# Spreading 48 row sums evenly over a hybrid encoder block, and splitting one job's first weights earlier

## The chip, the cores and the metric

The kernel runs on one core of one Trainium2 chip. A core has five engines that run side by side and wait for one another through semaphores: TensorE (PE: matmuls, with PEld its weight loads), VectorE (DVE), ScalarE (ACT), GpSimd (POOL) and SyncE (SP, which here only issues DMAs). The metric is the device time of one execution in microseconds, the median of several runs; lower is better.

## The reference

The reference is one layer of a bidirectional hybrid encoder block on 256 tokens of width 2048, all in fp32. A conditioning vector c gives six rows of modulation, and these are what the change is about:

```python
mod = silu(c) @ ada_w + ada_b                    # ada_w: 2048 x 12288
shift_m, scale_m, gate_m, shift_f, scale_f, gate_f = split(mod, 6)
h = rms_norm(x, norm_mix_w) * (1 + scale_m) + shift_m
proj = h @ w_in                                  # 2048 x 18512, split into the branches
y_a = (sigmoid(a_o) * rms_norm(mlstm(...))) @ w_branch_a   # 4 heads, both directions
y_b = (rms_norm(gated_delta(...)) * silu(b_z)) @ w_branch_b # 16 heads, both directions
x = x + gate_m * ((g_a * y_a + g_b * y_b) @ w_out)
hf = rms_norm(x, norm_ffn_w) * (1 + scale_f) + shift_f
x = x + gate_f * ((silu(hf @ w_gate) * (hf @ w_up)) @ w_down)
return rms_norm(x, norm_final_w)
```

Shift and scale of the mixer (parts 0 and 1 of mod) are needed at once; gate_m (part 2) after both branches, shift_f and scale_f (parts 3 and 4) before the FFN, gate_f (part 5) at the end.

## The kernel before

All weights are streamed from HBM once, in chunks of 1 MB. A chunk lands in one of three raw buffers. Half of it at a time is split into a rounded high part wh (a copy on ScalarE) and the rest wl (a subtraction on VectorE), three buffers each; TensorE then does three products per block, wh with the high activations, wh with the low ones, wl with the high ones. A job is a Python generator that does one such half per step: fjob (L173) for 128 output columns, two steps; tjob (L199) for 512 output columns, eight steps. A list called fills holds the jobs that aren't urgent, and fill(n) runs n of their steps; the latency chains of the two branches put such steps between their own.

The parts 2 to 5 of mod aren't computed on TensorE. For each of 16 blocks of a part a transposed block of ada_w, 128 rows of 2048 numbers (1 MB), is loaded (ask, L111) and multiplied with the row silu(c) and summed along the row in one VectorE instruction (add, L120). ask puts its load in SyncE's queue, the one that also loads the weight chunks. I call such an instruction a sum. Parts 2, 3 and 4 are 48 sums and are queued at L1016; part 5 is 16 sums during the FFN.

When a sum is traced is decided in pump (L157), which every step of every job calls. It has two ways. With the one buffer of the pool rows_p, a step asks for a load if none is out; a later step adds it if a sum is owed, more than two steps have gone by since the load, and the sums aren't held. With the variable every at 1 a sum is owed at each step, so this comes to one sum every four steps. The other way is taken while room (L108) names a pool of three buffers: then every fourth step traces one sum, and the loads run up to three ahead.

The stages in order, with what the sums do in them:

- start: norm, the first projections, and the gates; no sums of this kind.
- groups g = 0 to 3 of four gated-delta heads. For each, gdn_invert inverts small triangular blocks on VectorE (no sums), then come gdn_blocks and two pairs of heads, gdn_phase2 (L749), a chain of nine steps each, with the q, k, v jobs of the next group (b_job) and fills between the steps (L1040 on). every is 1 in these pairs, and the sums are held in steps 1 to 3 of a pair. A pair's last step transposes its output on TensorE (px), evicts it on ScalarE (obt) and stores it. After group g the job z of group g + 1 is put ahead of the fills (L1060), and the next inversion runs.
- in group 3 mLSTM heads 0 and 1 are begun; then every is set to 0 (L1121), and these heads end amid the y_b jobs. every is 1 again (L1147) for mLSTM heads 2 and 3, still amid y_b.
- y_a, four jobs, with room naming three buffers of a new pool sr and every at 4. That pool also holds gm and the products of row_diag (L1159), from which gate_m is spread over all partitions. merged (L1103) transposes the merged branches.
- the output jobs o, four, with sums called by hand at two steps of each and the rest of them at one step of the last (L1312). Then the FFN.

What order the engines run in is not the order of the program. The framework's planner simulates the program and gives each engine a fixed order: of the instructions that it believes ready, the one that was traced first. An instruction in order(...) is pinned behind the one traced before it on its engine. Functions in the list behind (settle, L139) are traced at the next half of a job; among them are the copies of a head's diagonal corners (corners, L676).

Of the kernel before, what the change touches and what calls it, by code (L numbers as in the profile page):

```python
# [15 lines left out]
P = 128  # L16
# [36 lines left out]
def hybrid_block(ctx: ExitStack, tc: tile.TileContext, xr, nfr, crow, pk_d, cst_d, ada2, ada4, win0, winb, wint, wba, wbb, wo, wgu, wd, out, dbg=None):  # L53
# [54 lines left out]
    room = [(rows_p, "ada", 1, 1)]  # L108
    asked, unasked, age = [], [], [0]

    def ask():  # L111

        pl, tag, bufs, _ = room[0]
        part, b = unasked.pop(0)
        raw = pl.tile([P, D], F32, tag=tag, bufs=bufs, name=f"ada{part}_{b}")
        order(nc.sync.dma_start(raw, ada4[part - 2, b]))
        asked.append((part, b, raw))
        age[0] = 0
# [80 lines left out]
    def tjob(name, chunks, xh, xl, done, early=0, by_token=None, steps=1, parts=((0, slice(0, 512)), (1, slice(0, 512)))):  # L199
# [7 lines left out]
        def halves(u, k0):  # L207
# [5 lines left out]
            order(S.activation(wh, raws[u][:, k0 : k0 + 2], AF.Copy), early)  # L213
            settle()
            order(V.tensor_tensor(wl, raws[u][:, k0 : k0 + 2], wh.bitcast(F32), ALU.subtract), early)  # L215
# [150 lines left out]
    def z_job(g, early=0):  # L366
# [4 lines left out]
        return tjob(f"z{g}", [wint[g, u] for u in range(4)], hh, hl, done, early)  # L371
# [654 lines left out]
    for g in range(4):  # L1026
# [94 lines left out]
    every[0] = owed[0] = 0  # L1121
# [25 lines left out]
    every[0] = 1  # L1147
# [32 lines left out]
    every[0] = 4  # L1180
    for g in range(4):
        for i, _ in enumerate(y_a(g)):
            if g and i == 3:
                merged(g - 1, mgh, mgl)
            if i in (1, 5) and g < 2:
                row_diag(2, 2 * g + i // 4, room[0][0])
            if i in (3, 7) and g < 2:
                row_spread(2, 2 * g + i // 4, gm)
    every[0] = 0
# [128 lines left out]
    room[0] = (rows_p, "ada", 1, 1)  # L1318
# [244 lines left out]
```

## Time and profile before

| | us |
|---|---|
| median of three runs | 1973.17 |
| lowest and highest | 1971.56, 1974.83 |
| the profiled execution | 1974.3 |
| its span, first to last instruction | 1972.4 |

The profile is of one execution. Its page gives busy times and their shares of the span; a chain of work, followed back from the last instruction to what released it; and groups of equal instructions with their count, mean duration in ns, and the idle time of the engine ahead of them. Other views answer from the same trace: who waited for whom, the instructions of one engine in order of time (start, length, engine, line, operation, with the idle time before it and its releaser in brackets), and windows with the busy time of each engine. SPq and ACTq rows are DMA issues of those queues, and their length reaches from the first to the last of the count. The end of a matmul is modelled, so matmuls overlap in these rows, and their rate is read from the starts.

### The profile page before, as it was taken

The numbers are of one execution on the slowest core, as the hardware profiler recorded it, in microseconds if no ns is written. First come the engines' busy times: TensorE is split into PE (matmuls) and PEld (weight loads), VectorE is DVE, ScalarE is ACT, GpSimd is POOL, SyncE is SP. The second block draws the span as 40 slices with busy tenths as digits, with TensorE's granted clock in tenths as the row PEclk, the third lists the DMA queues.
The fourth block names the chain that finished last, engine by engine and source line by source line (L and its number), as shares of the span: only waits on it lengthen the run. The fifth ranks groups of instructions, "written<-read, shape, count | busy, mean of one in ns | idle before, by whom it ended". The sixth has DMA issues, their size and how long they took to land.

```text
span 1972.4 us, 27079 instructions
## 1 busy us (share of the span) xinstructions
PE 1929.4 (98%) x10418; PEld 1703.5 (86%) x10418; DVE 1405.5 (71%) x2067; ACT 1030.0 (52%) x1555; POOL 116.5 (6%) x211
## 2 busy tenths in 40 slices
PE   8999999999999999999999999999999999999998
PEld 6878889998998899889787888888888888888886
DVE  6779887887888798866577878866665665555554
ACT  3137656764766577565544444644444444444444
POOL 0001210111001010110100000200000000000000
PEclk9999999999999999999999999999999999999999
DMA  9987676766566666586777888566676665565663
GB/s 399 420 349 226 184 249 240 252 214 208 203 217 213 237 218 229 192 296 246 277 282 266 323 317 330 191 252 238 238 265 241 237 238 205 197 213 197 208 199 142
DMA packets 78962, 485.64 MB, mean 246 GB/s; under 512 B 10585, under 2 KB 15969, under 8 KB 24433
## 3 DMA queue, kind: packets, MB, share of 16 engines
q1 hardware_dynamic: 63216, 450.69, 62.9%
q0 software_dynamic: 8160, 17.88, 4.5%
q10 hardware_dynamic: 7458, 15.36, 2.1%
q8 instruction: 81, 1.33, 0.3%
q14 instruction: 47, 0.39, 0.1%
HBM read 467.07 MB, written 16.82 MB: 245 GB/s over the span
## 4 chain that ended last, share of the span: by engine, by line
PE 81%; DVE 8%; DMA 6%; ACT 2%; issue 1%; POOL 0%; ACTq 0%; SPq 0%; DVEq 0%; POOLq 0%
PE acc_gt L234 4%; PE acc_gt L235 4%; PE acc_gt L236 4%; PE acc_up L236 4%; PE acc_up L235 4%; PE acc_up L234 4%; PE acc_d L236 4%; PE acc_d L235 4%; PE acc_d L234 4%; DMA ra<-ada 3%; PE acc_b L187 2%; PE acc_b L188 2%; PE acc_b L189 2%; PE acc_o L236 2%; PE acc_o L234 2%; PE acc_o L235 2%
## 5 line engine op out<-in xcount | busy, mean ns | idle before, releaser
L215 DVE TENSOR_TENSOR wl_d<-raw_d,wh_d 128x1024 fp32r<-128x1024 f32 x88 | 107.7, 1224 | 105.9 <-ACT wh_d L213 105.9
L215 DVE TENSOR_TENSOR wl_up<-raw_up,wh_up 128x1024 fp32r<-128x1024 f32 x88 | 107.7, 1224 | 100.2 <-ACT wh_up L213 100.1
L215 DVE TENSOR_TENSOR wl_gt<-raw_gt,wh_gt 128x1024 fp32r<-128x1024 f32 x88 | 108.1, 1229 | 80.2 <-ACT wh_gt L213 80.2
L187 PE MATMUL acc_b<-hh,wh_b 128*128 128x256 f32 x576 | 163.0, 283 | 0.6 <-ACT wh_b L182 0.6
L189 PE MATMUL acc_b<-hh,wl_b 128*128 128x256 f32 x576 | 159.6, 277 | 0.8 <-DVE wl_b L184 0.8
L188 PE MATMUL acc_b<-hl,wh_b 128*128 128x256 f32 x576 | 159.2, 276 | 0.0
L213 ACT ACTIVATE wh_d<-raw_d 128x1024 fp32r<-128x1024 f32 x88 | 92.9, 1056 | 126.5 <-PE acc_d L235 117.7
L213 ACT ACTIVATE wh_gt<-raw_gt 128x1024 fp32r<-128x1024 f32 x88 | 92.9, 1056 | 118.6 <-PE acc_gt L235 71.1
L213 ACT ACTIVATE wh_up<-raw_up 128x1024 fp32r<-128x1024 f32 x88 | 92.8, 1055 | 108.1 <-PE acc_up L235 77.1
L124 DVE SCALAR_TENSOR_TENSOR ada<-ada,crow 128x2048 f32<-128x2048 f32 x64 | 146.0, 2284 | 0.0
L234 PE MATMUL acc_gt<-wh_gt,hfh 128*128 128x512 f32 x352 | 135.6, 385 | 0.6 <-ACT hfh L1350 0.6
L235 PE MATMUL acc_gt<-wh_gt,hfl 128*128 128x512 f32 x352 | 134.9, 383 | 0.0
L236 PE MATMUL acc_gt<-wl_gt,hfh 128*128 128x512 f32 x352 | 134.1, 381 | 0.0
L234 PE MATMUL acc_up<-wh_up,hfh 128*128 128x512 f32 x352 | 133.4, 379 | 0.0
L235 PE MATMUL acc_up<-wh_up,hfl 128*128 128x512 f32 x352 | 133.4, 379 | 0.0
L236 PE MATMUL acc_up<-wl_up,hfh 128*128 128x512 f32 x352 | 133.4, 379 | 0.0
L234 PE MATMUL acc_d<-wh_d,ffh 128*128 128x512 f32 x344 | 130.5, 379 | 0.0
L235 PE MATMUL acc_d<-wh_d,ffl 128*128 128x512 f32 x344 | 130.5, 379 | 0.0
L236 PE MATMUL acc_d<-wl_d,ffh 128*128 128x512 f32 x344 | 130.4, 379 | 0.0
L561 PE MATMUL first<-x,raw 128*128 128x256 f32 x512 | 114.5, 382 | 7.2 <-ACT x L555 7.2
L561 PEld LDWEIGHTS first<-x,raw 128*128 128x128 f32 x512 | 96.0, 190 | 25.7 <-ACT x L555 13.3
L189 PEld LDWEIGHTS acc_b<-hh,wl_b 128*128 128x128 f32 x576 | 111.3, 193 | 1.0 <-DVE wl_b L184 1.0
(383 smaller groups left out, 5263.1 us busy)
## 6 DMA issues: line engine op xcount, KB each, us to landing
ada<-ada SPq DMA_DIRECT2D x64, 1024.0 KB, 6.0
raw_gt<-wgu SPq DMA_DIRECT2D x44, 1024.0 KB, 4.9
raw_up<-wgu SPq DMA_DIRECT2D x44, 1024.0 KB, 4.9
raw_d<-wd SPq DMA_DIRECT2D x44, 1024.0 KB, 4.9
raw_b<-winb SPq DMA_DIRECT2D x36, 1024.0 KB, 5.3
ra<-ada SPq DMA_DIRECT2D x32, 1025.0 KB, 15.8
raw<-win SPq DMA_DIRECT2D x16, 1024.0 KB, 14.5
raw_z<-wint SPq DMA_DIRECT2D x16, 1024.0 KB, 5.0
```

The source lines that it names most:

```text
L124: order(V.scalar_tensor_tensor(raw, raw, 1.0, row_c[:, :D], ALU.mult, ALU.mult, accum_out=mod[:, c : c + 1]))
L187: PE.matmul(o, wh[:, k], woven(hh[:, kk]), start=kk == 0, stop=False)
L188: PE.matmul(o, wh[:, k], woven(hl[:, kk]), start=False, stop=False)
L189: PE.matmul(o, wl[:, k], woven(hh[:, kk]), start=False, stop=kk == KB - 1)
L213: order(S.activation(wh, raws[u][:, k0 : k0 + 2], AF.Copy), early)
L215: order(V.tensor_tensor(wl, raws[u][:, k0 : k0 + 2], wh.bitcast(F32), ALU.subtract), early)
L234: order(PE.matmul(ps[t], xh[:, kk, c], woven(wh[:, k]), start=kk == 0, stop=False), early and steps > 1)
L235: PE.matmul(ps[t], xl[:, kk, c], woven(wh[:, k]), start=False, stop=False)
L236: PE.matmul(ps[t], xh[:, kk, c], woven(wl[:, k]), start=False, stop=kk == last)
L561: PE.matmul(first[o], raw[:, o], x[:, b], start=b == 0 and o % 2 == 0, stop=b == KB - 1 and o % 2 == 1)
```

## The change

The three-buffer way goes: room is removed, and the loads of all sums use the one buffer of rows_p. From the first pairs on, every stays 1 in group 3 and through the mLSTM heads, y_b, y_a and the output jobs, until the last output job, where whatever is left is added at its fourth step (fifth before). A new variable, calm, sets how many steps go by between a sum and the next load: 2 in the pairs of groups 0 to 2, 1 elsewhere. Since add now sets age to 0 as well, calm counts from the sum.

The z job of the next group is made at the last step of the second pair, ahead of that step, and its first half (the chunk's load, wh and wl) is traced there; the rest follows as before. The new argument pin = False leaves these two instructions to the planner, where a job with early halves would have pinned them. Tracing a half also traces what is in behind, so the corners of the last head now come ahead of the pair's last step.

```diff
-    room = [(rows_p, "ada", 1, 1)]
     def ask():
-        pl, tag, bufs, _ = room[0]
-        raw = pl.tile([P, D], F32, tag=tag, bufs=bufs, name=f"ada{part}_{b}")
+        raw = rows_p.tile([P, D], F32, tag="ada", name=f"ada{part}_{b}")
...
-    owed, held = [0], [False]
+    owed, held, calm = [0], [False], [1]
     def sums(n=1):
-            while unasked and len(asked) < room[0][3]:
+            if not asked:
                 ask()
...
-        if room[0][3] > 1:
-            if owed[0]:
-                owed[0] = 0
-                sums()
-        elif asked:
+        if asked:
             if owed[0] and age[0] > 2 and not held[0]:
-                owed[0] = 0
+                owed[0] = age[0] = 0
                 add()
-        elif unasked and every[0]:
+        elif unasked and every[0] and age[0] >= calm[0]:
             ask()
...
-            order(S.activation(wh, raws[u][:, k0 : k0 + 2], AF.Copy), early)
+            order(S.activation(wh, raws[u][:, k0 : k0 + 2], AF.Copy), early and pin)
             settle()
-            order(V.tensor_tensor(wl, ..., ALU.subtract), early)
+            order(V.tensor_tensor(wl, ..., ALU.subtract), early and pin)
...
         every[0] = 1
+        calm[0] = 2 if g < 3 else 1
...
+                if g < 3 and p and n == 9:
+                    zj = z_job(g + 1, 1, False)
+                    next(zj)
                 next(pairs[p], None)
...
-            fills.insert(0, z_job(g + 1))
+            fills.insert(0, zj)
             every[0] = owed[0] = 0
+            calm[0] = 1
...
-    every[0] = owed[0] = 0
+    held[0] = False
...
-    every[0] = 1
     drive(steps(mlstm(2), mlstm(3)), 3)
...
-    if asked:
-        add()
-    room[0] = (pool(sr_, "sr"), "sr", 3, 3)
-    gm = room[0][0].tile([P, D], F32, name="gm")
+    sr = pool(sr_, "sr")
+    gm = sr.tile([P, D], F32, name="gm")
...
-    every[0] = 4
...
-    every[0] = 0
...
-            if i in ((4, 7), (2, 5), (2, 5), (0, 2))[g]:
-                sums()
-            if g == 3 and i == 4:
+            if g == 3 and i == 3:
+                every[0] = owed[0] = 0
                 sums(P)
...
-    room[0] = (rows_p, "ada", 1, 1)
```

More of the change, by code (lines that the diff above doesn't have):

```diff
@@ L197, in woven, with tjob @@
         return a.rearrange("p (h c) -> p c h", h=n)
-    def tjob(name, chunks, xh, xl, done, early=0, by_token=None, steps=1, parts=((0, slice(0, 512)), (1, slice(0, 512)))):
+    def tjob(name, chunks, xh, xl, done, early=0, by_token=None, steps=1, pin=True, parts=((0, slice(0, 512)), (1, slice(0, 512)))):
         raws = {}
@@ L212, in halves @@
             wl = st.tile([P, 2, 512], F32R, tag="wl", bufs=3, name=f"wl_{name}_{u}_{k0}")
-            order(S.activation(wh, raws[u][:, k0 : k0 + 2], AF.Copy), early)
+            order(S.activation(wh, raws[u][:, k0 : k0 + 2], AF.Copy), early and pin)
             settle()
-            order(V.tensor_tensor(wl, raws[u][:, k0 : k0 + 2], wh.bitcast(F32), ALU.subtract), early)
+            order(V.tensor_tensor(wl, raws[u][:, k0 : k0 + 2], wh.bitcast(F32), ALU.subtract), early and pin)
             return wh, wl
@@ L364, in keep_f, with z_job @@
         return done
-    def z_job(g, early=0):
+    def z_job(g, early=0, pin=True):
         def done(ps):
@@ L370, in done @@
                 S.activation(szs[g][:, t], ps[t], AF.Silu)
-        return tjob(f"z{g}", [wint[g, u] for u in range(4)], hh, hl, done, early)
+        return tjob(f"z{g}", [wint[g, u] for u in range(4)], hh, hl, done, early, pin=pin)
     def b_job(h, j):
```

2 lines of the change are left out of this document (1 added, 1 removed).

## The prediction

> **What bounds the kernel now.** I read the page first: the busy times, the chain of work that ended last, and the group of the sums.
>
> ```profile
> span 1972.4 us, 27079 instructions
> PE 1929.4 (98%) x10418; PEld 1703.5 (86%) x10418; DVE 1405.5 (71%) x2067; ACT 1030.0 (52%) x1555; POOL 116.5 (6%) x211
> PE 81%; DVE 8%; DMA 6%; ACT 2%; issue 1%; POOL 0%; ACTq 0%; SPq 0%; DVEq 0%; POOLq 0%
> L124 DVE SCALAR_TENSOR_TENSOR ada<-ada,crow 128x2048 f32<-128x2048 f32 x64 | 146.0, 2284 | 0.0
> ```
>
> TensorE is busy for all but 43 us of the span, and the diff takes no matmul away and adds none. The 64 sums stay 64, at 2.28 us each. So the change can only move time through places where TensorE waits, and through the clock it is granted behind them. The second view is therefore the waits of TensorE alone, from the first sum to the start of the FFN (290 to 1255 us); its columns are the total, the number of waits and the longest.
>
> ```profile
> PE acc_ya L236 <- DVE wl_ya L215: 3.8, 2, 2.2
> PE vps L609 <- ACT vf L341: 2.7, 3, 1.4
> PE acc_z L234 <- ACT wh_z L213: 2.5, 1, 2.5
> PE acc_mb L236 <- DVE wl_mb L215: 1.8, 2, 1.0
> PE acc_ma L236 <- DVE wl_ma L215: 1.6, 2, 0.9
> PE acc_o L236 <- DVE wl_o L215: 1.1, 2, 0.8
> ...
> PE p L795 <- DVE pt L784: 0.2, 1, 0.2
> ```
>
> All rows of that answer together are 16.9 us, so this is nearly all that the change can win. Two rows are touched by the diff directly: acc_ya (3.8) and acc_z (2.5). The third view is the granted clock in windows of 3.41 us around these waits (columns: window, length, busy of PE, weight loads, DVE, ACT, POOL, then the clock, the DMA share and GB/s).
>
> ```profile
> 789.87:793.28 3.41, 1.03 (x7) 0.69 (x5) 2.92 (x11) 2.18 (x5) 0.20 (x1) 1.00 0.35 115
> 793.28:796.69 3.41, 3.24 (x7) 2.15 (x8) 1.86 (x2) 3.33 (x9) 1.97 (x4) 0.50 0.11 19
> 1083.41:1086.82 3.41, 1.26 (x7) 0.77 (x6) 3.41 (x5) 1.57 (x2) 0.00 (x0) 1.00 0.95 310
> 1086.82:1090.24 3.42, 3.42 (x10) 2.66 (x9) 3.18 (x4) 1.21 (x2) 0.00 (x0) 0.50 0.97 302
> 1097.07:1100.48 3.41, 2.17 (x11) 1.55 (x9) 2.06 (x3) 2.42 (x3) 0.00 (x0) 1.00 1.02 423
> ```
>
> Behind the window in which TensorE was busy for 1.03 us, and behind the one with 1.26 us, stands a window at half clock; at 0.50 over 3.42 us it does 1.7 us less work. Behind the one with 2.17 us there is none: matmuls that follow it, quoted below with the second wait, start 0.22 us apart. So a wait of 2 us or more costs about 1.7 us beyond itself.
>
> **The change part by part.**
>
> *The three-deep buffer goes; one sum every four steps runs through y_a.* In the kernel before, y_a opens with a burst: the leftover sum and then two more right behind it.
>
> ```profile
> 1078.58 2.28 DVE L124 SCALAR_TENSOR_TENSOR ada<-ada,crow 128x2048 f32<-128x2048 f32 x1
> 1080.80 2.29 DVE L124 SCALAR_TENSOR_TENSOR ada<-ada,crow 128x2048 f32<-128x2048 f32 x1
> 1083.01 2.28 DVE L124 SCALAR_TENSOR_TENSOR ada<-ada,crow 128x2048 f32<-128x2048 f32 x1
> ```
> ```profile
> 1086.49 0.93 PE L236 MATMUL acc_ya<-wl_ya,hah 128*128 128x512 f32 x2 [2.15 <-DVE wl_ya L215]
> ...
> 1100.90 0.70 PE L236 MATMUL acc_ya<-wl_ya,hah 128*128 128x512 f32 x2 [1.66 <-DVE wl_ya L215]
> 1101.43 0.38 PE L234 MATMUL acc_ya<-wh_ya,hah 128*128 128x512 f32 x1
> 1101.65 0.38 PE L235 MATMUL acc_ya<-wh_ya,hal 128*128 128x512 f32 x1
> ```
> ```profile
> 1069.74 3.39 SPq L116 DMA_DIRECT2D ada<-ada  x4
> 1083.12 2.54 SPq L116 DMA_DIRECT2D ada<-ada  x2
> 1085.75 0.60 SPq L210 DMA_DIRECT2D raw_ya<-wba  x1
> ```
> ```profile
> 1095.55 2.00 ACT L213 ACTIVATE wh_ya<-raw_ya 128x1024 fp32r<-128x1024 f32 x2 [4.90 <-DMA raw_ya<-wba]
> ```
>
> Three sums of 2.28 stand on VectorE ahead of one low half wl_ya, and TensorE waits 2.15 us for it. After the change the steps counted through the code put one sum at the third and one at the seventh of the eight steps of each y_a job, never two together. With one sum ahead 4.6 us of the VectorE queue are gone from that place, more than the wait: I take -2.15, and -1.7 for the half clock behind it. The bounds are the same and nothing. The second wait, 1.66 us, is a late weight chunk: four sum loads of 1 MB issued within 3.4 us stand ahead of raw_ya, two more issues hold SyncE for 2.5 us in front of the next, and ScalarE then stands 4.9 us for that chunk. With one load outstanding the row's 4.9 us has no cause left: -1.66, between that and nothing (VectorE also had its row_diag products in front there, which stay). What is late next in y_a is an ordinary sum ahead of one wl_ya, 2.28 us against weight buffers three deep.
>
> *The sums go on from the last pair through the mLSTM stage.* Counted step by step, the sums of the four group loops stay six each; behind them the kernel before has none until mLSTM heads 2 and 3, five there, one left over, ten in y_a and eight to the end of the output job. The changed one has nine up to the end of y_b, eight in y_a and seven in the output jobs. So four sums, 9.1 us of VectorE, come into the stretch 938 to 983, where VectorE was free.
>
> ```profile
> 938.00:983.00 45.00, 45.00 (x203) 35.35 (x202) 28.03 (x42) 26.69 (x46) 9.33 (x15) 1.00 0.75 264
> 983.00:1078.00 95.00, 94.96 (x435) 78.27 (x434) 68.71 (x96) 43.47 (x62) 0.53 (x1) 0.98 0.73 269
> 1078.00:1161.00 83.00, 79.19 (x370) 68.35 (x369) 68.41 (x72) 36.26 (x38) 0.00 (x0) 0.98 0.87 332
> ```
>
> 28.03 of 45 becomes 37.1, 83%; the stretch behind it, which holds five sums at just this cadence from one buffer, has 72% and TensorE busy for 94.96 of 95 us. Cost: nothing; the cover is the three wh and wl buffers. If it fails a sum stands in the path with 2.28 us, and that is the upper bound. In the output jobs two sums in each job stay two, and the emptying at the last one finds none left, so it costs nothing now (one sum, before).
>
> *One step more between a sum and the next load in groups 0 to 2.* The load that used to be asked for at the end of a group now comes at the first step of the next group's pairs, next to the q, k, v weights.
>
> ```profile
> ada<-ada SPq DMA_DIRECT2D x64, 1024.0 KB, 6.0
> raw_b<-winb SPq DMA_DIRECT2D x36, 1024.0 KB, 5.3
> ```
>
> A weight chunk behind it lands up to 6.0 us later; three raw buffers cover that, and group 0 of the kernel before already starts in this way. I take nothing, with a bound of +5.3 if one chunk is late. The first sum of each pair waits for the same held step as before, so the waits for vf (2.7 us) stay. A sum shifted by one step may win or lose the 0.3 us of a single wait in a pair's chain: nothing.
>
> *The z job's first half ahead of the last pair's end.* At the end of group 2 the high half stands behind the pair's last evictions.
>
> ```profile
> 790.94 0.84 ACT L845 ACTIVATE obt<-px,pk 128x256 f32<-128x256 f32 x2 [0.58 <-PE px L841]
> 792.30 1.06 ACT L213 ACTIVATE wh_z<-raw_z 128x1024 fp32r<-128x1024 f32 x1 [0.52 <-ACT obt L845]
> ```
> ```profile
> 429.80:491.80 62.00, 60.24 (x314) 53.11 (x313) 48.50 (x99) 30.36 (x40) 9.93 (x19) 1.00 0.67 219
> 613.20:674.90 61.70, 59.93 (x277) 51.80 (x276) 49.81 (x100) 33.59 (x46) 9.95 (x19) 1.00 0.72 236
> 790.90:856.10 65.20, 62.43 (x352) 55.83 (x351) 50.48 (x98) 36.39 (x50) 13.33 (x24) 0.97 0.69 227
> ```
>
> These three windows hold the same work, from the last pair's transposes to the first block product of the next group. Groups 0 and 1 had the z halves ready in time and take 62.0 and 61.7; group 2 takes 65.2, with its wait of 2.51 and its half clock. The best the edit can do is the difference, -3.5: what TensorE wins there it gives back in part, since groups 0 and 1 wait later for wl_mb, wl_ma and wl_o in these stretches. Only the first half is moved. It covers 2.6 us (12 matmuls at the 0.22 us between 1101.43 and 1101.65), and behind it stand the two evictions and what follows them on ScalarE's queue to 792.3, the diagonal corner copies that are now ordered ahead of the second half, some 1.7 us, and its own copy of 1.06: 4.1 us from 790.9. So about 1.5 us of the 2.51 may stay. I take -1.0 for the wait and -1.0 for better than even odds on the 1.7 us of half clock: -2.0, between 0 and -3.5. In groups 0 and 1 nothing, as their windows show no such loss. The load on SyncE's queue moves past nothing but the pair's last step, which issues none there.
>
> *The sum.* -2.15 - 1.7 - 1.66 - 2.0 = -7.5. For the new order I add +1.0, one wait of the size of the acc_mb and acc_ma rows at a place that I can't name. Net -6.5. The profiled execution took 1974.3 (its span and 1.9 around it), which gives 1967.8; the median of the runs is 1.1 lower, and against it the same sum gives 1966.7.
>
> **The rule that speaks against it.** The Trainium skill, "TensorE: Matmul & The Clock Gate", section "Why this matters for your kernels", says to keep TensorE from idling for more than about 3 us between bursts, and that one idle window puts the clock at half. By that rule waits of 2.15 and 2.51 us would not have caused the two half windows, they would come from elsewhere and stay, and the sum would be -6.5 + 2.7 = -3.8. The trace agrees with the page's Part 1 on the length of a window (3413 ns there, 3.42 us here), and not with the rule on the idle time: windows with 1.03 and 1.26 us of work in them were enough.
>
> **The rivals.** (a) The half clock windows stay, as mechanism of this kernel: they start wherever a fixed window happens to hold little work, and another falls on some thin place. Then 1.7 and 1.0 are not won: -3.8, 1969.4. For it: the second wait of y_a has none, so a wait alone doesn't make one. Against it: both stand right behind the two longest waits. (b) The time is given back: VectorE is the next limit in y_a (68.41 of 83), so the second wait stays for the row_diag products, and z wins nothing. -3.85 for the burst, +1.8 for new waits: 1971.1. For it: VectorE at 82% there. Against it: ten sums, 22.8 us, are in that time, and two go. (c) The edit at z does nothing, because the planner that orders each engine keeps the high half behind the evictions: 1968.7. For it: it isn't pinned. Against it: it is now traced ahead of them and ranks first.
>
> (d) Slower: SyncE's queue. A load can't issue before the last sum has freed the one buffer, and the chunks queued behind it wait too.
>
> ```profile
> SPq L116 <- DVE ada L124: 18.9, 4, 5.2
> ```
>
> That is the stretch 983 to 1078: 4.7 us a time. The price when a chunk comes too late is that of 1100.90 with its clock, 1.66 + 1.7 = 3.4. With 6.5 won elsewhere, the kernel is slower by more than 0.2% from four such waits among the 24 loads of the later stages on (13.4 - 6.5 = +6.9, 1980.1). Against it: in that very stretch loads wait like this and TensorE misses 0.04 us.
>
> **How the numbers follow.** 0.2% is 3.9 us, about what a measurement here tells from no change: below 1969.2 is faster, above 1977.1 slower. Forecast 0.50, (a) 0.10, (b) 0.19, (c) 0.08, (d) 0.13. Faster: 0.50 + 0.08 + 0.04 of (a) = 0.62; same: 0.19 + 0.06 = 0.25; slower 0.13. The range goes from 1962.5 (the sum with z at its bound, no new wait, and a wait or two of the pairs gone) to 1976, which takes in (a), (b), (c) and one late chunk; it leaves out most of (d). The forecast's own range is 1963 to 1969.
>
> **What would show it.** Right: no row of acc_ya waiting for wl_ya over 0.5 us, single sums about 10 us apart from the end of the pairs to the output jobs, no half clock in y_a, and a window from the last transposes of group 2 to the next block product of 62 to 63.5 us. Wrong: new rows of TensorE waiting for wl_yb, wl_ya or wl_o, or raw chunks of y_b ending ScalarE's idle time; half clock windows in new places; wh_z of group 2 still behind obt; group starts where wh_b waits for its chunk.

## The result, and the profile after

The changed kernel takes 1984.24 us in the median (1980.38 to 1986.07), the kernel before 1974.09 in the same comparison: a ratio of 1.0051, with a 95% interval from 1.0041 to 1.0062. It is slower by half a per cent, where I had forecast 1966.7. The profiled execution took 1983.31 us, its span 1981.4.

The page of the changed kernel, in the line of the busy times:

```profile
PE 1930.3 (97%) x10418; PEld 1702.5 (86%) x10418; DVE 1405.2 (71%) x2067; ACT 1031.8 (52%) x1556; POOL 116.8 (6%) x211
```

The work is the same on every engine to within 2 us, and the 64 sums still take 2.28 us each; the span is 9.0 us longer. So what came in is idle time and slow clock. The waits of TensorE from the first sum to the FFN (total, number, longest):

```profile
PE vps L603 <- ACT vf L335: 6.7, 8, 1.3
PE acc_z L230 <- DVE wl_z L209: 5.8, 2, 2.9
...
PE acc_z L228 <- ACT wh_z L207: 1.7, 1, 1.7
...
PE acc_yb L230 <- DVE wl_yb L209: 1.2, 2, 0.9
...
PE pxa L988 <- DVE hal L993: 0.7, 1, 0.7
```

The row of acc_ya, 3.8 us before, is gone. In its place vps (2.7 before) has grown by 4.0, and the z job, which waited 2.5 for its high halves, now waits 5.8 for low halves and 1.7 for a high one. Cut into stages, the difference is plain. The table is worked out from the traces; a stage ends where TensorE starts the first product of the next one, and the inversions begin at the end of the last pair's transposes. The first column is the length before, the others are differences to it, each from one profiled execution. Kernels e1 to e12 are the experiments below; what the four without a column (e4, e7, e11, e12) show stands with them. The rest of the FFN, behind these stages, is equal in all to 0.1 us.

| stage | before | after | e1 | e2 | e3 | e5 | e6 | e8 | e9 | e10 |
|---|---|---|---|---|---|---|---|---|---|---|
| up to the first pair | 314.7 | +0.6 | -0.2 | +1.2 | -1.0 | -1.2 | -0.2 | -1.2 | +0.1 | -1.8 |
| pairs of groups 0 to 2 | 352.5 | **+7.2** | -1.2 | +6.2 | +0.2 | -1.5 | -4.8 | +2.0 | -2.2 | -0.2 |
| inversion for group 1 | 62.0 | -0.4 | -0.1 | 0.0 | -0.6 | -0.1 | -0.5 | +0.4 | -0.1 | -0.1 |
| inversion for group 2 | 61.7 | **+4.7** | +0.2 | +0.5 | +4.5 | +0.4 | +4.4 | -0.1 | +0.3 | -0.1 |
| inversion for group 3 | 65.0 | +2.1 | -0.1 | +2.0 | +0.8 | -1.1 | +2.3 | +3.0 | +2.5 | -0.6 |
| pairs of group 3, mLSTM | 116.7 | +0.9 | +1.7 | +2.1 | +2.7 | +2.8 | 0.0 | 0.0 | +0.7 | +2.2 |
| y_b | 105.1 | +0.8 | +1.7 | +2.9 | -0.2 | +1.2 | -1.7 | 0.0 | +2.8 | -1.7 |
| y_a | 93.3 | **-6.1** | -6.1 | -6.1 | -6.1 | -6.1 | -1.7 | -5.3 | -6.1 | -5.9 |
| output jobs | 86.1 | -0.6 | -0.6 | -0.5 | -0.6 | -0.6 | 0.0 | +0.8 | +1.5 | +0.8 |
| norm ahead of the FFN | 23.3 | -0.3 | -0.1 | -0.1 | +0.4 | -1.7 | -1.1 | -1.0 | +25.2 | +1.1 |

Single windows at half clock (3.41 us long, 1.7 of it lost) fall in other places in each execution, so a difference of 2 us in one cell says little by itself. How far that goes is seen where a kernel changes nothing: e8 edits only y_a, and has +2.0 in the pairs and +3.0 in the inversion for group 3; e6 leaves all sums alone, and has -4.8 in the pairs. The bold ones are larger or stand in several kernels, and rows of waits go with them. What makes the +2.1 in the inversion for group 3 of the changed kernel isn't settled.

**y_a** went as forecast. The first 83 us of the stage, to half a microsecond, as a window (busy time of PE, weight loads, DVE, ACT, POOL, then clock, DMA share, GB/s), and the first and the last of its eight sums:

```profile
1093.01:1176.01 83.00, 83.00 (x398) 72.88 (x397) 68.70 (x73) 39.00 (x41) 0.00 (x0) 1.00 0.83 303
```
```profile
1095.86 2.28 DVE L122 SCALAR_TENSOR_TENSOR ada<-ada,crow 128x2048 f32<-128x2048 f32 x1
...
1173.01 2.28 DVE L122 SCALAR_TENSOR_TENSOR ada<-ada,crow 128x2048 f32<-128x2048 f32 x1
```

TensorE is busy for all 83.00 us at full clock (79.19 at 0.98 before), with eight single sums some 11 us apart.

**The pairs.** The second view of interest is VectorE's instructions in order, at the end of the first pair of group 0, with TensorE's late matmul behind them. In the changed kernel:

```profile
360.73 0.47 DVE L332 SCALAR_TENSOR_TENSOR cv<-pad,pk,cv 128x256 f32<-128x256 f32 x1
361.12 2.28 DVE L122 SCALAR_TENSOR_TENSOR ada<-ada,crow 128x2048 f32<-128x2048 f32 x1
...
363.33 0.48 DVE L332 SCALAR_TENSOR_TENSOR cv<-pad,pk,cv 128x256 f32<-128x256 f32 x1
...
365.38 0.48 DVE L332 SCALAR_TENSOR_TENSOR cv<-pad,pk,cv 128x256 f32<-128x256 f32 x1
...
366.36 0.44 PE L603 MATMUL vps<-cst,vf 128*128 128x128 f32 x2 [1.17 <-ACT vf L335]
```

and in the kernel before, where the same sum is the third of the pair too:

```profile
355.08 2.28 DVE L124 SCALAR_TENSOR_TENSOR ada<-ada,crow 128x2048 f32<-128x2048 f32 x1
...
358.42 0.48 DVE L338 SCALAR_TENSOR_TENSOR cv<-pad,pk,cv 128x256 f32<-128x256 f32 x1
...
361.19 0.46 DVE L338 SCALAR_TENSOR_TENSOR cv<-pad,pk,cv 128x256 f32<-128x256 f32 x1
```

The four cv instructions are the convolution of the next head's v. Before, the sum stood ahead of that chain; now it stands between its first and second links, the rest of the chain is put back by its 2.28 us, ScalarE's vf behind it is late, and TensorE waits 1.17 us. The same wait, 51 to 54 us behind the start of the pair, is new in five of the six pairs: 1.17, 0.71, 0.41, 0.62 and 1.16 us, which is nearly all of the 4.3 us by which TensorE is idle longer in the pairs. One more window at half clock adds 1.7, so that these account for 6.0 of the 7.2. The windows around the first of these waits, and around a wait in the next section, show what follows:

```profile
364.69:368.10 3.41, 2.24 (x16) 1.78 (x15) 1.32 (x3) 2.18 (x5) 0.00 (x0) 1.00 0.83 344
368.10:371.51 3.41, 3.41 (x10) 2.67 (x9) 2.69 (x12) 1.91 (x4) 0.00 (x0) 0.50 0.60 240
634.35:637.76 3.41, 0.61 (x3) 0.56 (x4) 3.13 (x11) 0.33 (x1) 0.00 (x0) 1.00 0.00 0
637.76:641.17 3.41, 3.41 (x10) 2.66 (x9) 3.20 (x9) 0.34 (x1) 0.00 (x0) 0.50 0.15 22
```

A wait of 1.17 us was enough for a window at half clock.

**The inversion for group 2.** The engines' instructions in order, after the second pair of group 1. Changed kernel:

```profile
621.57 2.18 POOL L657 DMA_DIRECT2D inst_d<-mi  x4 [15.71 <-DVE wl_z L209]
...
623.31 0.33 SPq L204 DMA_DIRECT2D raw_z<-wint  x1
...
628.19 12.27 SPq L204 DMA_DIRECT2D raw_ma<-wint  x2
...
628.21 0.52 POOL L664 DMA_DIRECT2D uu<-inst_d  x1 [4.46 <-DMA inst_d<-mi]
...
634.21 0.19 DVE L698 TENSOR_TENSOR utmp<-uu 64x30 f32<-64x30 f32 x1 [6.04 <-DMA uu<-inst_d]
...
637.15 0.48 PE L230 MATMUL acc_z<-wl_z,hh 128*128 128x512 f32 x1 [2.92 <-DVE wl_z L209]
```

Kernel before:

```profile
616.54 2.18 POOL L663 DMA_DIRECT2D inst_d<-mi  x4 [13.94 <-DVE wl_z L215]
...
618.70 0.33 SPq L210 DMA_DIRECT2D raw_z<-wint  x1
...
620.52 0.51 POOL L670 DMA_DIRECT2D uu<-inst_d  x1 [1.80 <-DMA inst_d<-mi]
...
623.16 7.62 SPq L210 DMA_DIRECT2D raw_ma<-wint  x2
...
624.52 0.20 DVE L704 TENSOR_TENSOR utmp<-uu 64x30 f32<-64x30 f32 x1 [1.39 <-DMA uu<-inst_d]
```

GpSimd stores four small blocks to DRAM (inst_d) and gathers them back (uu); VectorE inverts what comes. Before, the next weight chunk of z was issued 0.02 us ahead of the end of the fourth store's issue (618.70 against 616.54 + 2.18), and the stores were in 1.80 us later. Now it is issued 0.44 us ahead of that end (623.31 against 623.75). The stores are then in only after 4.46 us, the gather brings its data 6.0 us after its issue (634.21 - 628.21) and not 4.0 as before, and VectorE stands 6.04 us at its first product. The next chunk, raw_ma, was issued 2.64 us behind the gather before, and now stands 0.02 us ahead of it.

The traces also hold the start of every DMA packet, and these show both overtakings. Before, the last store's packets start 0.57 to 0.81 us behind the end of its issue, and the chunk of z begins at 0.94, behind them all. In the changed kernel the chunk begins at 0.52, 0.05 us ahead of where the store began before; the store's packets now start at 2.66 to 3.47, when 76 to 118 of the chunk's 128 have started. The other three stores aren't touched. The gather's first packet starts 2.2 us after its issue before, and 3.7 us after it in the changed kernel, by when 106 packets of raw_ma have started.

The low half of z is queued behind that product on VectorE, so TensorE waits 2.92 us and gets the half clock of 637.76.

### The profile page after: what moved, and what is told of

Same layout as the page of the kernel before. It is cut to its first block, busy times and chain, and to the rows that moved or that the text cites. A ratio compares the mean times of both kernels' runs of the same rounds, so it can differ in the third digit from the quotient of the medians.

```text
span 1981.4 us, 27080 instructions
## 1 busy us (share of the span) xinstructions
PE 1930.3 (97%) x10418; PEld 1702.5 (86%) x10418; DVE 1405.2 (71%) x2067; ACT 1031.8 (52%) x1556; POOL 116.8 (6%) x211
```

## The experiments

**The theory** that the trace suggests is that three things cost, each in its place: one step more before a load (calm at 2) in the pairs, the z edit in the inversions, and the sums in the mLSTM stage. **The rivals** are that one of them alone makes the loss and the others nothing, or that none does and the new order shifts waits and slow windows about. The first three experiments take the change apart.

### e1_late_only: the change with calm at 1 and the z job as before

```diff
-        calm[0] = 2 if g < 3 else 1
...
-                if g < 3 and p and n == 9:
-                    zj = z_job(g + 1, 1, False)
-                    next(zj)
...
-            fills.insert(0, zj)
+            fills.insert(0, z_job(g + 1))
```

> The changed kernel with two of its parts undone: calm stays 1 in the pairs of groups 0 to 2, and the z job is made where it was and has no early half. What is left is the one buffer and the cadence from the mLSTM stage to the output jobs. Theory A (three separate causes, read from the stage lengths of the two profiles: y_a -6.1, pairs of groups 0 to 2 +7.2, inversions 2 and 3 +6.8): the pairs and the inversions are as in the kernel before, y_a keeps its gain, y_b and the rest lose about 1, so 5 us below the kernel before, near 1969. Rival B (the planner's order shifts anywhere as soon as anything moves, and the losses aren't tied to a part): about as slow as the changed kernel in the pairs or inversions, +2 to +10.

Measured: 1969.42 us, a ratio of 0.9983 (0.9972 to 0.9993). What is left of the change makes the kernel faster. y_a and the output jobs give 6.65 us, and in this execution the mLSTM stage and y_b take 3.4 of it back (what of that is chance, e12 below tells).

### e2_calm2: the same with calm at 2 in groups 0 to 2

> The changed kernel with the z job made where it was and no early half; calm is 2 in the pairs as in the changed kernel. Theory A: the pairs lose their 7 us, by sums that land in front of the convolution chain of the next head (vps waiting for vf), the inversions lose nothing: +1 to +2 against the kernel before, near 1975.5. Rival B: inversions 2 and 3 are slow here too (+5 or more in them).

Measured: 1981.25 us, 1.0039 (1.0026 to 1.0052). One number in one line, against e1, costs 0.56% or 11 us. The pairs lose 6.2, and vps waits 6.8 us against 2.8 in e1. The loads don't show: from 16 us ahead of each group's first pair to the end of its second, ScalarE stands 1.3 us in all for late q, k, v chunks, and 3.1 in the kernel before.

### e3_z_early: the change with calm at 1

> The changed kernel with calm 1 throughout; the z job's first half is early as in the changed kernel. Theory A: the pairs are as in the kernel before, inversions 2 and 3 lose 4 to 7 us together (low halves of z stand on VectorE behind the first product of the inversion, which waits for its gathered triangles), y_a gains 6: between -2 and +1 against the kernel before. Rival B: the pairs lose as in the changed kernel.

Measured: 1974.64 us, 1.0002 (0.9991 to 1.0013). Against e1 the z edit costs 0.19%, 3.8 us, and its place is the inversion for group 2: +4.5. The pairs are as before. The three parts add up: -0.17% (e1), +0.19% for the z edit and +0.56% for calm at 2 make +0.58%, against the 0.51% of the whole change.

### e4_before_z: the kernel before with the early z half alone

```diff
+                if g < 3 and p and n == 9:
+                    zj = z_job(g + 1, 1, False)
+                    next(zj)
...
-            fills.insert(0, z_job(g + 1))
+            fills.insert(0, zj)
```

> The kernel before with the early half of z alone, not pinned; all sums as before. Theory A: only inversions 2 and 3 change, by +4 to +7 us, so near 1980. Rival (C: the early half does no harm by itself, it needs the later sums of calm 2 just ahead of the pair's end): within 2 us of the kernel before, or faster by the 3 that I had forecast for inversion 3.

Measured: 1979.21 us, 1.0025 (1.001 to 1.004), with a spread from 1972.9 to 1984.7. Slower again; but in the profiled execution, the fourth fastest of the ten, the inversion for group 2 was 0.4 us shorter than before, and that for group 3 longer by 2.8, no more than e8 has there without any edit. Its trace tells why the inversion for group 2 lost nothing: the chunk is issued 0.30 us ahead of the stores' end and the stores are in late, after 3.05 us, but raw_ma is issued 1.4 us behind the gather, which brings its data in 2.4 us. So the first race was half lost and the second one won. Where the slower executions lose their time isn't shown. The spread itself says little, since the kernel before goes from 1968.2 to 1978.9 in the same comparison.

### e5_corners_kept: e3, the copies of the corners left where they were

Tracing the half also traces what waits in behind, the copies of the last head's corners. Here they are put by, and traced at the next half as before:

```diff
                 if g < 3 and p and n == 9:
                     zj = z_job(g + 1, 1, False)
+                    late, behind[:] = behind[:], []
                     next(zj)
+                    behind[:] = late
```

> As the run with calm 1 throughout and z early, but tracing the early half leaves the corner copies of the last head where they were: behind the pair's output stores, with the second half of z. Theory A2 (the early half costs time only because the corners come ahead of the second output store on ScalarE's queue, the third copy of z then ends 0.45 us sooner, the next weight chunk is asked for at +5.0 instead of +5.5 us after the last transposes, gets ahead of the fourth small store of GpSimd, and the gather of the triangles lands 4 us later): inversion 2 back to 61.9 from 66.2, inversion 3 at 62 to 65, so 1967 to 1970, about the run with the later sums alone or up to 3 below. Rival D (it is the early half itself, through its place in the weight buffers): inversions 2 and 3 stay at 66 each, near 1974.6.

Measured: 1969.54 us, 0.9977 (0.9964 to 0.9989). The loss in the inversion for group 2 is gone (+0.4). The chunk is issued 0.03 us ahead of the stores' end, as before, and the rows in order of time are:

```profile
617.73 0.51 POOL L664 DMA_DIRECT2D uu<-inst_d  x1 [1.80 <-DMA inst_d<-mi]
...
622.11 0.19 DVE L698 TENSOR_TENSOR utmp<-uu 64x30 f32<-64x30 f32 x1 [1.77 <-DMA uu<-inst_d]
```

### e6_corners_only: the kernel before, the corners traced at the last step, no early z half

```diff
+                if g < 3 and p and n == 9:
+                    settle()
                 next(pairs[p], None)
```

> The kernel before, with everything that is put off traced just ahead of the last step of the second pair in groups 0 to 2, so that the corners come ahead of its output stores; no half of z is early and all sums are as before. Theory A2: the chunk is asked for 0.45 us sooner and the race with the fourth store is lost here too in inversion 2: +2 to +5 against the kernel before, 1976 to 1979. Rival D: nothing, within 1 of 1973.7.

Measured: 1981.59 us, 1.0031 (1.0017 to 1.0044). The corners alone make the loss, +4.4 in that inversion, with the same rows as in the changed kernel:

```profile
611.00 2.18 POOL L663 DMA_DIRECT2D inst_d<-mi  x4 [14.12 <-DVE wl_z L215]
...
612.74 0.33 SPq L210 DMA_DIRECT2D raw_z<-wint  x1
...
617.95 0.52 POOL L670 DMA_DIRECT2D uu<-inst_d  x1 [4.78 <-DMA inst_d<-mi]
```

The chunk is issued 0.44 us ahead of the stores' end (612.74 against 613.18). So of the z edit the early half does no harm in the inversion for group 2 (e5), and what it drags along does. The profiled execution is the fastest of the ten, at 1971.16, since its pairs and y_b came out short; the +4.4 is in it, but where the median loses its 0.31% can't be read from it.

The way there is on ScalarE's queue. In the kernel before, the corners (cc) stand behind both issues of the pair's output stores (ob_d):

```profile
613.77 0.82 ACTq L846 DMA_DIRECT2D ob_d<-obt  x2
614.64 0.26 ACT L679 ACTIVATE cc<-mi 32x64 f32<-32x64 f32 x1 [0.54 <-ACT obt L845]
```

and in e6 the second issue stands amid the corners:

```profile
608.87 0.26 ACT L679 ACTIVATE cc<-mb 32x64 f32<-32x64 f32 x1
608.94 0.33 ACTq L846 DMA_DIRECT2D ob_d<-obt  x1
```

ScalarE's idle 0.54 us is gone, and the high half behind the corners starts 2.6 us after the transposes' end and not 3.1. A raw buffer comes free as much earlier, and SyncE issues the next chunk.

All 14 traces agree on what that does (e11, which cuts the chunk, is told below). In the eight where the chunk is issued at most 0.04 us ahead of the stores' end (before, e1, e2, e5, e8, e9, e10, e12), the stores are in after 1.80 or 1.81 us; with 0.30 us (e4) they are in after 3.05; with 0.44 (the changed kernel, e3, e6, e7) after 4.41 to 4.78. In the inversion for group 3 a chunk issued 0.2 us ahead (e5, e10) delays nothing: 1.74.

### e7_pinned: e3 with the early half pinned in order

```diff
-                    zj = z_job(g + 1, 1, False)
+                    zj = z_job(g + 1, 1)
```

> As the run with calm 1 throughout and z early, but the copy and the subtraction of the early half are pinned in program order. Theory A2: pinning moves the half of z back to its place in the program and leaves the corners ahead of the stores, so the race is lost as without it: near 1974.6, within 3. Rival E (the loss comes from the half floating ahead without the pin): back to 1969 to 1971.

Measured: 1979.15 us, 1.0022 (1.0013 to 1.0032). The three inversions lose 3.1, 7.3 and 3.3, and the low halves of z are waited for all along:

```profile
PE acc_z L230 <- DVE wl_z L209: 15.0, 13, 3.1
```

Leaving the half to the planner is the better of the two.

### e8_burst_less_one: the kernel before, one sum less at the start of y_a

```diff
-    every[0] = 4
+    every[0], owed[0] = 4, 0
```

> The kernel before with one sum taken out of the burst at the start of y_a (the owed mark is cleared there, so the first sum from the three buffers comes some steps later). Theory A (the 6.1 us of y_a are the burst: a wait of 2.15 for the low half behind three sums, the half clock behind it, and 1.66 for a late chunk): with two sums in place of three the first wait and its half clock go, -3.8, the second wait may stay since the four loads still go out together: y_a at 88 to 90 instead of 93.3, near 1970. Rival F (it is the loads alone that starve y_a): y_a stays at 92 or more.

Measured: 1969.71 us, 0.998 (0.9968 to 0.9991). Two sums stand together where there were three, with the three buffers as before, and four loads still issued together ahead of them (3.48 us from the first to the last):

```profile
1082.68 2.28 DVE L124 SCALAR_TENSOR_TENSOR ada<-ada,crow 128x2048 f32<-128x2048 f32 x1
...
1084.89 2.28 DVE L124 SCALAR_TENSOR_TENSOR ada<-ada,crow 128x2048 f32<-128x2048 f32 x1
```

y_a is shorter by 5.3 us and TensorE waits for nothing in it. One assignment gives most of what the whole new cadence gives.

### e9_calm2_held: e2 with the sums held off in the last two steps of a pair

By now two theories of calm at 2 stood against each other: the third sum of a pair, moved from step 7 to step 8, into the convolution; or the load, asked for a step later, beside the q, k, v weights.

```diff
-                held[0] = n < 4
+                held[0] = n < 4 or g < 3 and n > 7
```

> e2 (the sums as in the changed kernel, the z job as before) with the sums held off in steps 8 and 9 of each pair of groups 0 to 2 too. Theory: the loss in the pairs is the third sum of a pair, which one step more has moved from step 7 to step 8 and there onto VectorE amid the convolution chain of the next head. Held off, that sum is gone from there: the waits of TensorE for vf go back from 6.8 us to about 2.8, and the stretches of pair 0.0, 2.0 and the third inversion, +1.4, +2.5 and +2.0 in e2, come back to the kernel before within 0.7. Each group then does four sums and not six, so about six more are left for the emptying at the last output job, 14 us of VectorE there, of which TensorE may wait for 5 to 12. Total therefore near e2 or a few us above, 1975 to 1985, while the pairs are cured. Rival: the loss comes from the loads being asked for a step later, beside the q, k, v weights (the term of my prediction with its bound of 5.3 us); then the pairs stay 5 us longer and the vf row stays at 6 to 7.

Measured: 1998.64 us, 1.0127 (1.0107 to 1.0147). The first row is e2's, the second that of e9:

```profile
PE vps L603 <- ACT vf L335: 6.8, 8, 1.4
```
```profile
PE vps L603 <- ACT vf L335: 2.6, 3, 1.4
```

The pairs are cured: the first pairs of groups 0 and 2 are within 0.01 us of the kernel before, where e2 had lost 1.4 and 2.5. But e9 takes away more than the third sum. In the first pair of group 0 the second load is still asked for later, 28.8 us behind the start and not 27.7. The third load of a pair isn't asked for at all, since the buffer stays full until the next pair, and so none falls at the start of a group either. So e9 by itself doesn't part sum and load. The traces do: the new waits of e2 stand behind vf, right behind the third sum, and ScalarE stands no longer for chunks than before. So it is the third sum's place. Two parts of what I expected fell. The inversion for group 3 didn't come back (+2.5). And the sums left over for the last output job, some six, cost 25 us and not 5 to 12. With one buffer, the last three of them wait some 5 us each for their loads, as this one does, and TensorE waits 24.5 us for what stands behind them:

```profile
1265.39 2.32 DVE L122 SCALAR_TENSOR_TENSOR ada<-ada,crow 128x2048 f32<-128x2048 f32 x1 [5.02 <-DMA ada<-ada]
```

### e10_both_clean: the kernel before with only what won

The early z half as in e5, with the corners kept, and the assignment of e8; no new cadence.

> The kernel before with only what the runs showed to win: the z job's first half early and unpinned with the corner copies left where they were (as in e5), and the sum that opens y_a taken from the burst (as in e8); the cadence in the pairs and in the mLSTM stage as before. Theory: y_a -5.3 as in e8, the third inversion -1 as in e5, nothing lost in the pairs or in y_b: 1967 to 1969, ratio about 0.9965, below e5 and e8. Rival: the race of the inversion's small stores with the weight chunk is lost or won by chance whatever is traced, and the z half wins nothing: as e8, 1969.7 or 0.998, with a wider spread.

Measured: 1967.60 us (1963.33 to 1969.48), 0.9963 (0.9949 to 0.9977), the fastest of all in the median, by its ratio 7.3 us under the kernel before (the interval overlaps those of e1, e5 and e8). Of the group 3 inversion's wait for wh_z, 2.51 us, this is left:

```profile
789.20 0.48 PE L234 MATMUL acc_z<-wh_z,hh 128*128 128x512 f32 x1 [0.45 <-ACT wh_z L213]
...
791.79 0.70 PE L236 MATMUL acc_z<-wl_z,hh 128*128 128x512 f32 x2 [1.46 <-DVE wl_z L215]
```

### e11_chunk_cut: e3, that one weight chunk cut to an eighth

The chunk of z that is issued early is here loaded in 16 of 128 partitions, and the third chunk is split twice, so z of group 2 is computed from other weights.

```diff
-                nc.sync.dma_start(raws[u], chunks[u])
+                cut = name == "z2" and u == 3
+                part = 16 if cut else P
+                nc.sync.dma_start(raws[u][:part], chunks[u][:part])
+                if cut:
+                    raws[u] = raws[2]
```

> e3 (corners ahead of the stores, second inversion 66.2 us, the fourth small store landing at +9.3 us after the transposes' end) with one thing taken away: of the weight chunk that is issued 0.4 us earlier there, the fourth of job z of group 2, only 16 of 128 partitions are loaded (128 KB and not 1 MB), and the job splits the third chunk a second time in its place, so z of group 2 is computed from other weights. All instructions before it stay. Theory (the chunk's packets delay GpSimd's fourth store): the store lands at +6.7 to +7.5, the gather is issued by +8.2, VectorE's first product comes at +11 to +12 and the stretch goes back to 61.5 to 62.5 us. Rival (the corner copies or ScalarE's earlier halves delay the store or the gather in another way): the store still lands after +9 and the stretch stays at 65 to 67 us.

Measured: one execution, 1970.88 us, beside one of the kernel before with 1977.51. In order of time:

```profile
612.27 2.18 POOL L661 DMA_DIRECT2D inst_d<-mi  x4 [14.12 <-DVE wl_z L213]
...
614.01 0.34 SPq L206 DMA_DIRECT2D raw_z<-wint  x1
...
616.72 12.22 SPq L206 DMA_DIRECT2D raw_ma<-wint  x2
...
617.51 0.52 POOL L668 DMA_DIRECT2D uu<-inst_d  x1 [3.06 <-DMA inst_d<-mi]
```

Between the two expectations. Issued at the same moment (0.44 us ahead of the stores' end), the smaller chunk holds the stores up less, 3.06 us against 4.46 in the changed kernel and 1.80 undisturbed, and the stretch is 64.15 us against 66.2 in e3 and 61.7 before. So the delay goes with the chunk's bytes, as the theory says, but I had expected all of it to go and half is left. The packet starts part the two halves of the rest. The 16 packets of the small chunk still start ahead of the last store's, which come 0.5 us later than undisturbed, and the stores' landing is later by 1.3; raw_ma's first packet starts only after that landing. The gather then takes 5.2 us and not 4.0 as before: raw_ma, issued 0.8 us ahead of it, now stands where the changed kernel had it too.

### e12_mlstm_sums: the kernel before, the sums not switched off in the mLSTM stage

```diff
     o4s = [o_load(g) for g in range(2)]
-    every[0] = owed[0] = 0
+    held[0] = False
```

> The kernel before with one thing of the change: the sums aren't switched off between the last pairs and mLSTM heads 2 and 3, so some four more stand in that stage and as many fewer are left at the last output job; the three buffers and the burst in y_a stay, and so do calm and the z job. Theory (these sums cost what the eight kernels with the new cadence lose in the pairs of group 3, the mLSTM stage and y_b): these stages together +2 to +4.5 us against the kernel before, rows of wl_yb, hal or hs among TensorE's waits there, total 1974 to 1979. Rival (the loss comes from elsewhere in the new cadence, or is scatter): these stages between -1.7 and +0.5 as in the four kernels with the old cadence, and a total within 0.1% of before.

Measured: 1976.92 us, 1.0016 (1.0006 to 1.0026). The pairs of group 3, the mLSTM stage and y_b together are longer by 4.6 us in the profiled execution, and no other stage by more than 1.3. Only a part of that is waits; TensorE waits 1.0 us in the stretch, in these rows:

```profile
PE pxa L994 <- DVE hal L999: 0.8, 1, 0.8
PE acc_yb L236 <- DVE wl_yb L215: 0.2, 1, 0.2
```

The rest is half clock: 10.2 us of it in this stretch (three windows), against 3.4 in the kernel before (one), 3.4 more work lost. So theory and rival each have a part, the waits and the scatter.

The windows at half clock in this stretch follow no wait at all. The kernel before, TensorE's instructions in order of time and then two windows:

```profile
1022.04 2.73 PE L962 MATMUL pden<-ones,mdec 128*128 128x1 f32 x24
```
```profile
1022.00:1025.41 3.41, 3.41 (x29) 3.30 (x29) 2.50 (x8) 1.40 (x3) 0.00 (x0) 1.00 0.86 322
1025.41:1028.82 3.41, 3.41 (x10) 2.65 (x9) 1.13 (x2) 0.00 (x0) 0.00 (x0) 0.50 0.88 269
```

and the changed kernel, with the window that holds the larger part of the run; neither it nor the next is at half clock:

```profile
1039.62 2.73 PE L956 MATMUL pden<-ones,mdec 128*128 128x1 f32 x24
```
```profile
1040.52:1043.93 3.41, 3.41 (x25) 3.22 (x25) 2.50 (x8) 0.49 (x3) 0.00 (x0) 1.00 0.73 243
```

pden is a run of 24 matmuls of one column each, 2.6 us long: TensorE counts as busy all the time, and computes one column where the matmuls around it compute 512 in 0.22 us. The stretch has two such runs in every kernel. Worked out from the starts and the borders of the windows for all 14 traces: in 12 of the 28 runs at least 2.19 us of the run lie in one window of 3.41 us, and the next window is at half clock in all of them; in 14 a border cuts the run so that less than 2.0 us lie in either window (0.9 and 1.7 at 1040.52), and none is. Two runs have 2.0 in one window, one with half clock behind it (e1) and one without (e3).

## Why the prediction was wrong

**The burst in y_a: right.** Forecast -2.15, -1.7 and -1.66, together -5.5; the stage is 6.1 us shorter, no row of acc_ya is left, and e8 shows that the count of sums together was the cause of the first wait. That the second wait came from the four loads isn't shown: it is gone in e8 too, where the three buffers and the four loads remain.

**The step that failed: "One step more between a sum and the next load in groups 0 to 2 ... I take nothing".** It cost about 11 us in the times (e2 against e1). In the changed kernel's trace 7.2 us are in the pairs, and where the rest went is open. I had looked at the load, with +5.3 as the bound for a late chunk, and no chunk was later: ScalarE stood 1.3 us for q, k, v chunks in e2 and 2.2 in the changed kernel, in the stretches where it stood 3.1 before. The sentence "A sum shifted by one step may win or lose the 0.3 us of a single wait in a pair's chain" held the right object and the wrong size: what is queued behind the sum on VectorE is a chain of four dependent links that ends in a matmul, and the wait is that of the sum less its slack, 0.4 to 1.2 us in five pairs, with a half clock window where it falls badly. The rows of VectorE around the third sum of a pair, in the trace before, would have shown how little lies between it and that chain.

**The z job: the -2.0 was too large, and a thing beside it was costed at nothing.** I had estimated that 1.5 of the 2.51 us would stay; in e10 it is 1.91, 0.45 on the high half and 1.46 on the low one. The half clock window of the stretch is gone in e10 and e5, as I had hoped, but a wait for wl_a behind it, 0.2 us in the kernel before, is 1.8 and 1.3 there, so the stretch gains 0.6 and 1.1. That wait isn't the z edit's alone: e8 has 1.9. In the changed kernel itself the stretch is 67.1 us and not 62 to 63.5, with waits of 1.7 for wh_z and 2.9 for wl_z. The corners I had named only as an item on ScalarE's queue in group 2, and "In groups 0 and 1 nothing" is the line that failed: in group 1 they moved a weight chunk 0.4 us forward, ahead of GpSimd's last store, and the inversion for group 2 became 4.7 us longer. "The load on SyncE's queue moves past nothing" was true of the load that the diff moves and not of the next one, which follows when its buffer comes free.

**The sums in the mLSTM stage: "Cost: nothing" was wrong, by about its bound.** TensorE's waits from the pairs of group 3 to y_a add up to less than 0.1 us in the kernel before, and also in e4, e6 and e8 with the old cadence (1.6 in e10); with the sums running on they are 2.4 in the changed kernel, 1.4 in e1, 3.7 in e2, 2.1 in e3, 4.4 in e5, 2.4 in e7, 2.7 in e9, 2.1 in e11 and 1.0 in e12. Most of it stands in the row that I had given as the sign of failure, wl_yb, and in hal and hs beside it. The mean is 2.5, about the bound that I had given, one sum of 2.28. The half clock in this stage, none to three windows, goes by where a window's border cuts the pden runs, and no edit aims at that.

**The clock: "a wait of 2 us or more costs about 1.7 us beyond itself" was too simple.** The trace before had a case against it: its window from 578.24 us holds 2.02 us of work, with a wait for vf of 1.39, and the next is at half clock. In the changed kernel a window with 2.24 us of work, with a wait of 1.17, was followed by half clock; one with 2.17 in the trace before was not; and one that was busy for all its 3.41 us, mostly with one-column matmuls, was. So it seems to be little work in a window, of whatever kind, and not the wait alone; where the limit lies these windows don't tell. The Trainium skill's rule ("TensorE: Matmul & The Clock Gate", "Why this matters for your kernels") of keeping idle times under about 3 us is again not borne out: 1.17 us was enough, and with pden none. Where a window's border falls I can't tell before a run, and an edit shouldn't be credited with one.

**The rivals.** (d) had the right sign, for the most part for other reasons. Late chunks of y_b did come, as it said: from mLSTM to the end of y_b ScalarE stands 8.8 us for raw_yb in the changed kernel and 1.8 in the kernel before, and 7.4 in e12. Little of that reaches TensorE, whose waits for wl_yb there are 0.92 and 0.32 us, both with a sum just ahead on VectorE; how much of them is the sum and how much the late chunk isn't parted. In y_a and the output jobs ScalarE waits for no chunk at all, where it had stood 7.9 us before. (a) held in so far as the windows only moved. (b) and (c) fell: y_a kept its gain, and the z half does run ahead. I had looked for the loss in the stages where sums were added, and most of it came in the stages where they were only shifted.

## What to carry to other kernels

A filler instruction that is shifted by one step needs the same look as one that is added: read on its engine what it now stands ahead of, and whether a chain that ends in a matmul runs there. When work is made earlier, follow the buffer that it frees to the next load on the queue, and see whose small transfer that load now gets ahead of. And where a few instructions stand together in one place, take one of them from that place before changing the cadence everywhere: e8 is one assignment and won as much as all of the new cadence without its faults (e1).

## What the runs showed of the hardware that I had not expected

TensorE's clock fell to half behind 2.7 us of one-column matmuls without a single wait (e12's rows), or stayed, as a border of the windows of 3.41 us happened to cut the run. Neither the chain of waits nor the busy time shows such a place.

A weight load of 1 MB issued 0.4 us earlier kept the last of four small stores on another queue from being in for 4.5 instead of 1.8 us, and with the next load ahead of it the gather behind them took 6.0 instead of 4.0; cut to 128 KB the first load still cost the stores 1.3 us. The Trainium skill ("DMA: Bandwidth & Descriptors", "Queues, rings and completion order") says that each DMA engine takes turns between the queues that have work for it, packet by packet. The starts in the trace show that 76 of the load's 128 packets went first in the changed kernel, and that none did in the kernel before, where the load began 0.13 us behind the store's last. They don't tell which of the 16 DMA engines a packet ran on, so the turns themselves aren't shown; what they left the small store with was a wait of some 2.7 us.
